# Sums of x's squares: from channel-major tiles with GpSimd additions to token-major tiles with ScalarE's accumulator, in one layer of a three-branch decoder block

## The chip, the cores and the metric

The kernel runs on one core of a Trainium2 chip. The metric is device time in microseconds (us). The time before is 1533.58 us, the median of three runs (1532.06 to 1534.87).

## The reference, cut to what matters

One decoder layer over 512 tokens of width 2048: RMSNorm of x, one wide projection `w_in`, three token mixers (sliding-window attention A, forgetting attention B, cross-attention C into 256 normalised memory tokens), gates, a merge and an output projection, all in float32.

```python
def rms_norm(x, gain):
    x32 = x.astype(jnp.float32)
    y = x32 * lax.rsqrt(jnp.mean(x32 * x32, axis=-1, keepdims=True) + EPS)
    return (y * gain.astype(jnp.float32)).astype(x.dtype)
...
    hn = rms_norm(x, norm_gain)
    proj = hn @ w_in
    (qa, ka, va, za, qb, kb, vb, zb, fb, qc, zc, gate_logits) = jnp.split(proj, IN_OFFSETS, axis=-1)
...
    mkv = rms_norm(mem, mem_norm_gain) @ w_mem_kv
...
    y = g[:, :, 0] * ua + g[:, :, 1] * ub + g[:, :, 2] * uc
    return x + y @ w_out
```

What the change touches is the mean of x's squares per token, and when the things around it happen.

## The kernel before, in words

**Tiling.** Every float32 product is made of three matmuls on split operands: high part times high part, high times low, low times high. For x the high part is `ah` (ScalarE, `x_part`, L307) and the low part `al` (VectorE, L308); for a weight tile `wa` the high part is `wb` (ScalarE, L195) and the low part `wc` (VectorE, L198). Both x and the weights come from DRAM on the queue of SyncE (SP).

**Units.** The projection runs in column chunks: qB, kB and vB of the first half of branch B come first, then others. A chunk is eight units; a unit is 256 of the 2048 channels: 24 matmuls of 384 columns (396 in kB, which carries the forget gates too). In the eight units of qB, unit u also brings x's tile `xraw` for its channels (`load_x`, channel-major: 128 channels by 512 tokens, twice). `xraw` has three buffers, `wa`, `wb` and `wc` two each. Gain is applied with x; the factor 1/rms of a token (`rstd`) is applied later, on what comes out of the projection, so the matmuls do not wait for it.

**Order.** PE, VectorE, ScalarE and GpSimd execute in the order in which the program is written. A clock counts half a slot for three matmuls, so that a unit is 4 slots; `later(dt, f)` and `at_slot(t, f)` put f's instructions into the order when that clock is reached. qB takes slots 0 to 32, kB 32 to 64, vB 64 to 96. The load of unit u+1 (`st.load`) is written at the start of unit u. SyncE's queue is ordered by the compiler's scheduler; each of its transfers waits for its buffer, and those behind it wait too.

**Sums of squares.** In each unit of qB ScalarE squares the whole `xraw` tile into `xsq` (L340) and GpSimd adds it to the accumulator `acc` (L341). `x_norm` at slot 36.5 sums `acc` over partitions with small matmuls against a column of ones (`x_ss`, L350) and takes the power -1/2. `x_rows` (slot 52) spreads `rstd` into rows (`rstdb`). `mem_norm` squares the memory's token-major tiles on ScalarE with its accumulator (`accum_out`, L373). `late_constants`, at slot 20, issues the loads of gains, sinks, the bias table and the like, 14 small transfers. `plan_sums` (slot 58 on) builds combinations of x's quarters (`x3s` to `x6s`, VectorE L1003, L1006, L1021) for a later stage.

Of the kernel before, what the change touches and what calls it, by code (L numbers as in the profile page):

```python
# [19 lines left out]
P = 128  # L20
# [23 lines left out]
def tile_hybrid_block(ctx, tc, xT, x, memT, mem, ng, mng, w_in, b_forget, gqa, gka, sinks, gqb, gkb, gqc, gkc,  # L44
# [41 lines left out]
    ac.activation(relt[:, :8], mhalf, AF.Exp)  # L86

    def late_constants():
        sy.dma_start(out=mngt, in_=mng)
        sy.dma_start(out=bfor, in_=b_forget.partition_broadcast(P))  # L90
        sy.dma_start(out=nsink, in_=sinks.partition_broadcast(P))
        later(20, lambda: po.tensor_scalar(nsink, nsink, -1.0, None, op0=ALU.mult))
        sy.dma_start(out=relt, in_=relm)
        for name, g, d in (("qa", gqa, 64), ("ka", gka, 64), ("qb", gqb, 64), ("kb", gkb, 64), ("qc", gqc, 128), ("kc", gkc, 128)):
            t = cp.tile([P, 1], F32, name=f"g_{name}")
            for o in range(0, P, d):
                sy.dma_start(out=t[o:o + d, :], in_=g)
            if name[0] == "q":
                t2 = cp.tile([P, 1], F32, name=f"gs_{name}")
                later(20, lambda t=t, t2=t2, d=d: ve.tensor_scalar(t2, t, float(np.float32(d) ** np.float32(-0.5)), None,  # L100
                                                                   op0=ALU.mult))
                t = t2
            gains[name] = t

    nsink = cp.tile([P, 12], F32, name="nsink")
    bfor = cp.tile([P, 12], F32, name="bfor")
# [15 lines left out]
    def at_slot(t, f):  # L122

        heapq.heappush(agenda, (t, next(seq), f))

    def later(dt, f):
        at_slot(clock[0] + dt, f)
# [172 lines left out]
    early = tc.tile_pool(name="early", bufs=1)  # L300
    earlyp = early.__enter__()

    acc = earlyp.tile([P, UK, S], F32, name="acc")

    def x_part(u, t, k):
        g = ngt[:, u * UK + k:u * UK + k + 1]
        ac.activation(ah[u][:, k, :], t[:, k, :], AF.Copy, scale=g)  # L307
# [3 lines left out]
    def first_unit(segs):  # L311

        (w, c0, n), = segs
        raw, h, l = w_tile("a", F32), w_tile("b"), w_tile("c")
        t = earlyp.tile([P, UK, S], F32, tag="xraw", bufs=3, name="xraw0")
        res = []
        for k in range(UK):
            sy.dma_start(out=t[:, k, :], in_=xT[k * P:(k + 1) * P, :])
            sy.dma_start(out=raw[:, k, :n], in_=w[k * P:(k + 1) * P, c0:c0 + n])
        for k in range(UK):  # L320
            hi, lo = h[:, k, :], l[:, k, :]
            low = x_part(0, t, k)
            ve.tensor_copy(hi[:, :n], raw[:, k, :n])
            ve.tensor_sub(lo[:, :n], raw[:, k, :n], f32(hi[:, :n]))
            low()
            res.append((hi, lo, n))
        later(1, lambda: ac.activation(acc, t, AF.Square))
        return res

    def load_x(u):  # L330
        if u == 0:
            return
        t = earlyp.tile([P, UK, S], F32, tag="xraw", bufs=3, name=f"xraw{u}")
        sy.dma_start(out=t, in_=xT[u * UK * P:(u + 1) * UK * P, :].rearrange("(k p) n -> p k n", p=P))
        for k in range(UK):
            x_part(u, t, k)()
        sq = earlyp.tile([P, UK, S], F32, tag="xsq", bufs=2, name=f"xsq{u}")

        def square():
            ac.activation(sq, t, AF.Square)  # L340
            po.tensor_tensor(acc, acc, sq, op=ALU.add)  # L341
        later(1.5, square)

    def x_norm():
        ones = earlyp.tile([P, 2], F32, name="ones")
        po.memset(ones, 1.0)
        b = sbank("x_ss")
        ve.tensor_tensor(acc[:, 0, :], acc[:, 0, :], acc[:, 1, :], op=ALU.add)
        for t in range(NT):
            pe.matmul(b[:, 2 * t:2 * t + 2], acc[:, 0, t * P:(t + 1) * P], ones, start=(t == 0), stop=(t == NT - 1))  # L350
        v = earlyp.tile([P, NT], F32, name="v_x")
        ve.tensor_scalar(v, b[:, :2 * NT].rearrange("p (t c) -> p t c", c=2)[:, :, 0], 1.0 / D, EPS, op0=ALU.mult, op1=ALU.add)
        power(rstd, v, NT)
        later(2, lambda: ve.scalar_tensor_tensor(out=rstd2, in0=rstd, scalar=1.0 / 64, in1=rstd, op0=ALU.mult, op1=ALU.mult))

    def x_rows():
        bb = earlyp.tile([P, NT, P], F32, name="rstd_cols")
# [6 lines left out]
    def power(out_ap, v, n):  # L364
        po.tensor_tensor(out_ap, v, mhalf[:, :n], op=ALU.pow)

    def mem_norm(t0):
        ss = earlyp.tile([P, 2, 2], F32, name="ss_m")

        def load(t, c):  # L370
            r = earlyp.tile([P, 1024], F32, tag="xtok", bufs=2, name=f"xt{t}{c}")
            sy.dma_start(out=r, in_=mem[t * P:(t + 1) * P, c * 1024:(c + 1) * 1024])
            later(10, lambda: ac.activation(r, r, AF.Square, accum_out=ss[:, t, c:c + 1]))  # L373

        def finish():
            v = earlyp.tile([P, 2], F32, name="v_m")
            ve.tensor_tensor(v, ss[:, :, 0], ss[:, :, 1], op=ALU.add)
            ve.tensor_scalar(v, v, 1.0 / D, EPS, op0=ALU.mult, op1=ALU.add)
            power(mrstd, v, 2)
        for k in range(4):  # L380
            at_slot(t0 + 6 * k, lambda k=k: load(k // 2, k % 2))
        at_slot(t0 + 32, finish)


    def qk_tile(name, tag, n, bufs):
# [30 lines left out]
    def evac_qk(key, tag, n, hd, bufs, scale=rstd, nt=NT, after=None, wait=0.5):  # L416

        nh = n // hd
        state = {}

        def f(b, pb, c0=0):
            if after is not None:
                after(b, pb)
            if b == 0:
                state["t"] = tokp.tile([P, nt, n], F32, tag=tag, bufs=bufs, name=f"t_{key}")
            t = state["t"]
            if scale is None:
                ac.copy(t[:, b, :], pb[:, c0:c0 + n])
            else:
                ac.activation(t[:, b, :], pb[:, c0:c0 + n], AF.Copy, scale=scale[:, b:b + 1])  # L430
            normalise(t[:, b, :], nh, hd, f"{key}{b}", wait, b if scale is None else None)
            if b == nt - 1:
                toks[key] = t
        return f
# [80 lines left out]
    def sbank(name):  # L515
        return bank(1, name)
# [331 lines left out]
    def b_chunks(part):  # L848
        c = part * 384
        st.add(f"qB{part}", [(w_in, QB + c, 384)], "tok", act_x, KT,  # L850
               evac_qk(f"qB{part}", "tq", 384, 64, 2, **({} if part else {"scale": None, "wait": 12})),
               None if part else load_x)
        segs = [(w_in, KB + c, 384)] + ([] if part else [(w_in, FB, 12)])
        st.add(f"kB{part}", segs, "tok", act_x, KT, evac_qk(f"kB{part}", "tk", 384, 64, 1, after=None if part else evac_f))
        st.add(f"vB{part}", [(w_in, VB + c, 384)], "tok", act_x, KT, evac_v(f"vB{part}", 6))
# [152 lines left out]
    def plan_sums(t0):  # L1008


        def one(u, n):
            xa, xb = (place(i, f"x{i}s{u}").rearrange("p k (t n) -> p (k t) n", t=2) for i in (n, n + 1))
            a, s1, s2, d = (xa[:, i, :] for i in range(4))
            s3, c, s4, b = (xb[:, i, :] for i in range(4))
            rows = [slice((2 * u + k) * P, (2 * u + k + 1) * P) for k in range(2)]
            halves = [slice(0, 256), slice(256, 512)]
            for dst, k, h in ((a, 0, 0), (b, 0, 1), (c, 1, 0), (d, 1, 1)):
                sy.dma_start(out=dst, in_=xT[rows[k], halves[h]])

            def norm(dst, k, h):  # L1020
                ve.scalar_tensor_tensor(out=dst, in0=dst, scalar=ngt[:, 2 * u + k:2 * u + k + 1],  # L1021
                                        in1=rstdb[:, halves[h]], op0=ALU.mult, op1=ALU.mult)

            def store():
                r = slice(u * P, (u + 1) * P)
                sy.dma_start(out=xad[r, :].rearrange("p (k n) -> p k n", n=256), in_=xa)
                sy.dma_start(out=xbd[r, :].rearrange("p (k n) -> p k n", n=256), in_=xb[:, 0:3, :])
            steps = [lambda: (norm(a, 0, 0), norm(b, 0, 1)), lambda: (norm(c, 1, 0), norm(d, 1, 1)),
                     lambda: (add(s1, b, d), sub(s2, s1, a)), lambda: (sub(s3, a, b), sub(s4, c, s2)), store]
            for i, f in enumerate(steps):  # L1030
                later(5.5 + 1.5 * i, f)
        for u in range(NP):
            at_slot(t0 + (0, 9, 18, 27, 44, 72, 100, 128)[u], lambda u=u: one(u, 3 + 2 * (u % 2)))
# [405 lines left out]
    for _ in range(5):  # L1439
        pe.matmul(wb, wz[:, :P], wz, start=True, stop=True)  # L1440
    st.load(1)
    at_slot(20, late_constants)
    at_slot(36.5, x_norm)
    run(0, 8)
    mem_norm(clock[0] + 4)
    later(20, x_rows)
    plan_sums(clock[0] + 26)
    run(8, n_p1)
    early.__exit__(None, None, None)
    atp = tc.tile_pool(name="at", bufs=1)  # L1450
    at.p = atp.__enter__()
# [64 lines left out]
```

## Time and profile before

| what | value |
|---|---|
| median of three runs | 1533.58 us |
| the profiled execution: its own time | 1534.17 us |
| the profiled execution: its span in the trace | 1532.4 us |
| PE busy in the span | 1492.3 us (97%) |
| VectorE (DVE), ScalarE (ACT), GpSimd (POOL) busy | 1083.6, 721.6, 272.0 us |
| chain that ended last | PE 73%, DVE 11%, ACT 6%, DMA 5% |

The span is what the trace covers; the execution's own time is 1.8 us longer, and that execution lies 0.6 us over the median. Busy times of PE are modelled ends of pipelined matmuls, so a wait read between two starts is a little longer than the idle time that a row names.

### The profile page before, as it was taken

The page shows a single profiled execution, that of the slowest core. Times are in us where ns is not written, and L with a number is a line of the kernel's source. Part 1 is how long each engine was busy: PE and PEld are TensorE (multiplying, and loading weights), DVE is VectorE, ACT ScalarE, POOL GpSimd, SP SyncE. Part 2 cuts the span into 40 slices and gives each one's busy share as a digit, 9 for nine tenths or more (in the row PEclk, how much of TensorE's full clock was granted, in tenths as well). Part 3 has the DMA queues.
Part 4 walks back from the last instruction along what each step waited for, and adds up shares of the span by engine and source line. Part 5 has one row for each costly group of instructions (what it writes and reads, how often), then busy time and mean ns, then how long its engine had stood idle before and what let it go on. Part 6 is the DMA issues. An engine that isn't in the chain of part 4 may idle for free.

```text
span 1532.4 us, 20507 instructions
## 1 busy us (share of the span) xinstructions
PE 1492.3 (97%) x7233; PEld 1273.4 (83%) x7233; DVE 1083.6 (71%) x1818; ACT 721.6 (47%) x1198; POOL 272.0 (18%) x295
## 2 busy tenths in 40 slices
PE   8999999999999999999999999999999999999998
PEld 7999999998877888888887878787878788887876
DVE  7576765663577764568878877777777556589987
ACT  5434654663566654454444444435355322245432
POOL 3323760662225431200000000000000101110000
PEclk9999999999999999999999999999999999999999
DMA  6656433223244322476666676767676756567583
GB/s 198 172 187 207 122 109 111 84 76 93 83 146 158 99 72 78 162 235 210 210 202 221 206 230 197 243 192 246 193 228 208 278 194 198 173 229 259 191 294 140
DMA packets 125264, 273.23 MB, mean 178 GB/s; under 512 B 13916, under 2 KB 52956, under 8 KB 125160
## 3 DMA queue, kind: packets, MB, share of 16 engines
q1 hardware_dynamic: 120984, 257.22, 52.6%
q10 hardware_dynamic: 4176, 14.69, 3.0%
q8 instruction: 57, 0.93, 0.2%
q14 instruction: 47, 0.39, 0.1%
HBM read 240.39 MB, written 31.48 MB: 177 GB/s over the span
## 4 chain that ended last, share of the span: by engine, by line
PE 73%; DVE 11%; ACT 6%; DMA 5%; issue 3%; POOL 1%; ACTq 1%; SPq 0%; DVEq 0%; POOLq 0%
PE P L1069 27%; PE z L284 11%; PE uA L1069 4%; PE qA L284 4%; PE kB L284 3%; PE qB L284 3%; PE uB L1069 3%; PE kvA L284 3%; PE uC L1069 3%; DMA rawl<-in_w_in_dram 3%; PE qC L284 3%; PE vB L284 2%; DVE R L1003 2%; DVE rawl L1006 2%; DVE wd L1112 2%
## 5 line engine op out<-in xcount | busy, mean ns | idle before, releaser
L1109 ACT CAST wa<-rawl 128x1024 fp32r<-128x1024 f32 x128 | 134.7, 1052 | 256.2 <-PE P L1069 140.1
L198 DVE TENSOR_TENSOR wc<-wa,wb 128x512 fp32r<-128x512 f32 (+2 forms) x254 | 162.0, 664 | 109.3 <-ACT wb L195 108.7
L195 ACT CAST wb<-wa 128x512 fp32r<-128x512 f32 (+2 forms) x254 | 131.3, 565 | 143.8 <-PE z L284 48.3
L1006 DVE TENSOR_TENSOR rawl<-rawl 128x512 f32<-128x512 f32 x256 | 176.6, 690 | 26.6 <-DMA rawl<-in_w_in_dram 16.5
L1112 DVE TENSOR_TENSOR wc<-rawl,wa 128x1024 fp32r<-128x1024 f32 x128 | 156.3, 1221 | 50.8 <-ACT wa L1109 50.7
L1350 POOL TENSOR_TENSOR y<-y,gA 128x512 f32<-128x512 f32 x16 | 24.8, 1559 | 701.0 <-DVE gA L1348 700.4
L1109 ACT CAST wb<-rawl 128x512 fp32r<-128x512 f32 (+1 forms) x128 | 107.1, 837 | 74.7 <-PE P L1069 51.7
L1112 DVE TENSOR_TENSOR wd<-rawl,wb 128x512 fp32r<-128x512 f32 (+1 forms) x128 | 121.8, 952 | 12.9 <-ACT wb L1109 12.7
L284 PE MATMUL z<-ah,wb 128*128 128x512 f32 x256 | 102.2, 399 | 0.0
L284 PE MATMUL z<-ah,wc 128*128 128x512 f32 x256 | 100.0, 391 | 0.0
L284 PE MATMUL z<-al,wb 128*128 128x512 f32 x256 | 99.8, 390 | 0.0
L1069 PE MATMUL P<-wd,xhx 128*128 128x512 f32 x192 | 76.5, 398 | 4.0 <-DVE wd L1112 3.6
L1069 PE MATMUL P<-wb,xhx 128*128 128x512 f32 x192 | 75.9, 395 | 1.8 <-ACT wb L1109 1.0
L1069 PE MATMUL P<-wb,xlx 128*128 128x512 f32 x192 | 74.9, 390 | 0.0
L1069 PE MATMUL P<-wa,xlx 128*128 128x512 f32 x192 | 74.7, 389 | 0.0
L1069 PE MATMUL P<-wa,xhx 128*128 128x512 f32 x192 | 74.7, 389 | 0.0
L1069 PE MATMUL P<-wa,yhx 128*128 128x512 f32 x192 | 74.7, 389 | 0.0
L1069 PE MATMUL P<-wa,ylx 128*128 128x512 f32 x192 | 74.7, 389 | 0.0
L1069 PE MATMUL P<-wc,yhx 128*128 128x512 f32 x192 | 74.7, 389 | 0.0
L1069 PE MATMUL P<-wc,xhx 128*128 128x512 f32 x192 | 74.7, 389 | 0.0
L1003 DVE TENSOR_TENSOR R<-P,R 128x512 f32<-128x512 f32 x88 | 56.1, 684 | 20.6 <-PE P L1069 20.2
L574 POOL TENSOR_SCALAR pB<-pB,denB 128x128 f32<-128x128 f32 (+3 forms) x48 | 56.1, 1169 | 49.1 <-DVE denB L573 34.5
(384 smaller groups left out, 4022.1 us busy)
## 6 DMA issues: line engine op xcount, KB each, us to landing
rawl<-in_w_in_dram SPq DMA_DIRECT2D x144, 512.0 KB, 4.4
rawl<-in_w_out_dram SPq DMA_DIRECT2D x48, 512.0 KB, 4.7
wa<-in_w_in_dram SPq DMA_DIRECT2D x63, 384.0 KB, 3.3
wa<-in_w_in_dram SPq DMA_DIRECT2D x64, 256.0 KB, 3.1
rawl<-in_w_in_dram SPq DMA_DIRECT2D x48, 256.0 KB, 4.2
gates<-R ACTq DMA_DIRECT2D x24, 512.0 KB, 7.9
wa<-in_w_in_dram SPq DMA_DIRECT2D x16, 512.0 KB, 3.7
wa<-in_w_mem_dram SPq DMA_DIRECT2D x16, 512.0 KB, 3.4
```

The source lines that it names most:

```text
L195: ac.copy(hi[:, :n], raw[:, i, :n])
L198: ve.tensor_sub(lo[:, :n], raw[:, i, :n], f32(hi[:, :n]))
L284: pe.matmul(pb, a, m, start=b in fresh, stop=last and not todo[b])
L574: po.tensor_scalar(p, p, den[:, 4 + i:5 + i], None, op0=ALU.mult)
L1003: ve.tensor_tensor(out, a, b, op=ALU.add)
L1006: ve.tensor_tensor(out, a, b, op=ALU.subtract)
L1069: pe.matmul(*args, **kw)
L1109: ac.copy(hi[:, :k, :], src)
L1112: return lambda: ve.tensor_tensor(lo[:, :k, :], src, f32(hi[:, :k, :]), op=ALU.subtract)
L1350: po.tensor_tensor(y, y, g, op=ALU.add)
```

## The change

The squares leave the qB units: `acc`, `xsq`, GpSimd's additions and the small matmuls are gone. Instead eight token-major tiles of x (128 tokens by 1024 channels, `xt`, four buffers) are loaded from the row-major x, one every 3 slots from slot 20, and ScalarE squares each 6 slots later with its accumulator (`square_sums`); `root` adds the two halves per token at slot 49. `late_constants` goes from slot 20 to slot 40 and spreads its loads, 3 slots apart. `mem_norm` goes from slot 36 to 60, `x_rows` from 52 to 56, `plan_sums` from 58 to 60, and the normalisation of qB's output waits 25 slots instead of 12.

```diff
@@ -86,21 +86,24 @@
     ac.activation(relt[:, :8], mhalf, AF.Exp)
 
     def late_constants():
-        sy.dma_start(out=mngt, in_=mng)
-        sy.dma_start(out=bfor, in_=b_forget.partition_broadcast(P))
-        sy.dma_start(out=nsink, in_=sinks.partition_broadcast(P))
-        later(20, lambda: po.tensor_scalar(nsink, nsink, -1.0, None, op0=ALU.mult))
-        sy.dma_start(out=relt, in_=relm)
-        for name, g, d in (("qa", gqa, 64), ("ka", gka, 64), ("qb", gqb, 64), ("kb", gkb, 64), ("qc", gqc, 128), ("kc", gkc, 128)):
+        def gain(name, g, d):
             t = cp.tile([P, 1], F32, name=f"g_{name}")
             for o in range(0, P, d):
                 sy.dma_start(out=t[o:o + d, :], in_=g)
             if name[0] == "q":
                 t2 = cp.tile([P, 1], F32, name=f"gs_{name}")
-                later(20, lambda t=t, t2=t2, d=d: ve.tensor_scalar(t2, t, float(np.float32(d) ** np.float32(-0.5)), None,
-                                                                   op0=ALU.mult))
+                later(8, lambda t=t, t2=t2: ve.tensor_scalar(t2, t, float(np.float32(d) ** np.float32(-0.5)), None, op0=ALU.mult))
                 t = t2
             gains[name] = t
+
+        steps = [lambda: sy.dma_start(out=bfor, in_=b_forget.partition_broadcast(P))]
+        steps += [lambda a=a: gain(*a) for a in (("qb", gqb, 64), ("kb", gkb, 64))]
+        steps += [lambda: sy.dma_start(out=nsink, in_=sinks.partition_broadcast(P)),
+                  lambda: sy.dma_start(out=relt, in_=relm), lambda: sy.dma_start(out=mngt, in_=mng),
+                  lambda: po.tensor_scalar(nsink, nsink, -1.0, None, op0=ALU.mult)]
+        steps += [lambda a=a: gain(*a) for a in (("qa", gqa, 64), ("ka", gka, 64), ("qc", gqc, 128), ("kc", gkc, 128))]
+        for i, f in enumerate(steps):
+            later(3 * i, f)
 
     nsink = cp.tile([P, 12], F32, name="nsink")
     bfor = cp.tile([P, 12], F32, name="bfor")
@@ -300,8 +303,6 @@
     early = tc.tile_pool(name="early", bufs=1)
     earlyp = early.__enter__()
 
-    acc = earlyp.tile([P, UK, S], F32, name="acc")
-
     def x_part(u, t, k):
         g = ngt[:, u * UK + k:u * UK + k + 1]
         ac.activation(ah[u][:, k, :], t[:, k, :], AF.Copy, scale=g)
@@ -324,7 +325,6 @@
             ve.tensor_sub(lo[:, :n], raw[:, k, :n], f32(hi[:, :n]))
             low()
             res.append((hi, lo, n))
-        later(1, lambda: ac.activation(acc, t, AF.Square))
         return res
 
     def load_x(u):
@@ -334,24 +334,26 @@
         sy.dma_start(out=t, in_=xT[u * UK * P:(u + 1) * UK * P, :].rearrange("(k p) n -> p k n", p=P))
         for k in range(UK):
             x_part(u, t, k)()
-        sq = earlyp.tile([P, UK, S], F32, tag="xsq", bufs=2, name=f"xsq{u}")
-
-        def square():
-            ac.activation(sq, t, AF.Square)
-            po.tensor_tensor(acc, acc, sq, op=ALU.add)
-        later(1.5, square)
-
-    def x_norm():
-        ones = earlyp.tile([P, 2], F32, name="ones")
-        po.memset(ones, 1.0)
-        b = sbank("x_ss")
-        ve.tensor_tensor(acc[:, 0, :], acc[:, 0, :], acc[:, 1, :], op=ALU.add)
-        for t in range(NT):
-            pe.matmul(b[:, 2 * t:2 * t + 2], acc[:, 0, t * P:(t + 1) * P], ones, start=(t == 0), stop=(t == NT - 1))
-        v = earlyp.tile([P, NT], F32, name="v_x")
-        ve.tensor_scalar(v, b[:, :2 * NT].rearrange("p (t c) -> p t c", c=2)[:, :, 0], 1.0 / D, EPS, op0=ALU.mult, op1=ALU.add)
-        power(rstd, v, NT)
-        later(2, lambda: ve.scalar_tensor_tensor(out=rstd2, in0=rstd, scalar=1.0 / 64, in1=rstd, op0=ALU.mult, op1=ALU.mult))
+
+    def square_sums(src, t, c, ss):
+
+        r = earlyp.tile([P, 1024], F32, tag="xtok", bufs=4, name=f"xt{t}{c}")
+        sy.dma_start(out=r, in_=src[t * P:(t + 1) * P, c * 1024:(c + 1) * 1024])
+        later(6, lambda: ac.activation(r, r, AF.Square, accum_out=ss[:, t, c:c + 1]))
+
+    def root(ss, out_ap, n):
+        v = earlyp.tile([P, n], F32, name=f"v_{n}")
+        ve.tensor_tensor(v, ss[:, :, 0], ss[:, :, 1], op=ALU.add)
+        ve.tensor_scalar(v, v, 1.0 / D, EPS, op0=ALU.mult, op1=ALU.add)
+        power(out_ap, v, n)
+
+    def x_norm(t0):
+        ss = earlyp.tile([P, NT, 2], F32, name="ss_x")
+        for n in range(2 * NT):
+            at_slot(t0 + 3 * n, lambda n=n: square_sums(x, n // 2, n % 2, ss))
+        at_slot(t0 + 6 * NT + 5, lambda: root(ss, rstd, NT))
+        at_slot(t0 + 6 * NT + 7, lambda: ve.scalar_tensor_tensor(out=rstd2, in0=rstd, scalar=1.0 / 64, in1=rstd, op0=ALU.mult,
+                                                                 op1=ALU.mult))
 
     def x_rows():
         bb = earlyp.tile([P, NT, P], F32, name="rstd_cols")
@@ -366,20 +368,9 @@
 
     def mem_norm(t0):
         ss = earlyp.tile([P, 2, 2], F32, name="ss_m")
-
-        def load(t, c):
-            r = earlyp.tile([P, 1024], F32, tag="xtok", bufs=2, name=f"xt{t}{c}")
-            sy.dma_start(out=r, in_=mem[t * P:(t + 1) * P, c * 1024:(c + 1) * 1024])
-            later(10, lambda: ac.activation(r, r, AF.Square, accum_out=ss[:, t, c:c + 1]))
-
-        def finish():
-            v = earlyp.tile([P, 2], F32, name="v_m")
-            ve.tensor_tensor(v, ss[:, :, 0], ss[:, :, 1], op=ALU.add)
-            ve.tensor_scalar(v, v, 1.0 / D, EPS, op0=ALU.mult, op1=ALU.add)
-            power(mrstd, v, 2)
         for k in range(4):
-            at_slot(t0 + 6 * k, lambda k=k: load(k // 2, k % 2))
-        at_slot(t0 + 32, finish)
+            at_slot(t0 + 4 * k, lambda k=k: square_sums(mem, k // 2, k % 2, ss))
+        at_slot(t0 + 24, lambda: root(ss, mrstd, 2))
 
 
     def qk_tile(name, tag, n, bufs):
@@ -848,7 +839,7 @@
     def b_chunks(part):
         c = part * 384
         st.add(f"qB{part}", [(w_in, QB + c, 384)], "tok", act_x, KT,
-               evac_qk(f"qB{part}", "tq", 384, 64, 2, **({} if part else {"scale": None, "wait": 12})),
+               evac_qk(f"qB{part}", "tq", 384, 64, 2, **({} if part else {"scale": None, "wait": 25})),
                None if part else load_x)
         segs = [(w_in, KB + c, 384)] + ([] if part else [(w_in, FB, 12)])
         st.add(f"kB{part}", segs, "tok", act_x, KT, evac_qk(f"kB{part}", "tk", 384, 64, 1, after=None if part else evac_f))
@@ -1439,13 +1430,12 @@
     for _ in range(5):
         pe.matmul(wb, wz[:, :P], wz, start=True, stop=True)
     st.load(1)
-    at_slot(20, late_constants)
-    at_slot(36.5, x_norm)
-    run(0, 8)
-    mem_norm(clock[0] + 4)
-    later(20, x_rows)
-    plan_sums(clock[0] + 26)
-    run(8, n_p1)
+    at_slot(40, late_constants)
+    x_norm(20)
+    at_slot(56, x_rows)
+    mem_norm(60)
+    plan_sums(60)
+    run(0, n_p1)
     early.__exit__(None, None, None)
     atp = tc.tile_pool(name="at", bufs=1)
     at.p = atp.__enter__()
```

How the order moves, at three places. First ScalarE, in the program before, in the second and third unit of qB (`ah` x's high part, `wb` the weights' high part, `xsq` the squares):

```order
L307 ACTIVATE ah_74<-xraw_136,ngt 128x512 x2
L195 CAST wb_145<-wa_143 128x384 x2
L327 ACTIVATE acc<-xraw_123 128x1024
L340 ACTIVATE xsq_142<-xraw_136 128x1024
L307 ACTIVATE ah_75<-xraw_182,ngt 128x512 x2
L195 CAST wb_191<-wa_189 128x384 x2
```

and of the change, from the seventh unit of qB to the first of kB:

```order
L308 ACTIVATE ah_79<-xraw_333,ngt 128x512 x2
L198 CAST wb_341<-wa_339 128x384 x2
L308 ACTIVATE ah_80<-xraw_373,ngt 128x512 x2
L198 CAST wb_381<-wa_379 128x384 x2
L342 ACTIVATE xt_331,ss_x<-xt_331 128x1024
L198 CAST wb_417<-wa_414 128x396 x2
```

Ahead of those rows the changed ScalarE holds only `ah` and `wb` rows; the squares of x begin behind the last `wb` of qB, from other tiles, `xt`.

Then SyncE's queue, in the program before, from the sixth unit's weights on (`nsink`, `relt` and `g_` are the constants, `xraw` x's channel-major tiles, `wa` weights):

```order
L185 DMA wa_312<-in_w_in_dram 128x2x384
L91 DMA nsink<-in_sinks_dram 128x12
L93 DMA relt<-in_relm_dram 128x256
L97 DMA g_qa<-in_gqa_dram 64x1 x2
L97 DMA g_ka<-in_gka_dram 64x1 x2
L97 DMA g_qb<-in_gqb_dram 64x1 x2
L97 DMA g_kb<-in_gkb_dram 64x1 x2
L97 DMA g_qc<-in_gqc_dram 128x1
L97 DMA g_kc<-in_gkc_dram 128x1
L334 DMA xraw_369<-in_xT_dram 128x2x512
L185 DMA wa_376<-in_w_in_dram 128x2x384
L334 DMA xraw_410<-in_xT_dram 128x2x512
```

and in the change, from the same weights on:

```order
L188 DMA wa_299<-in_w_in_dram 128x2x384
L341 DMA xt_331<-in_x_dram 128x1024
L334 DMA xraw_333<-in_xT_dram 128x2x512
L188 DMA wa_339<-in_w_in_dram 128x2x384
L341 DMA xt_365<-in_x_dram 128x1024
L334 DMA xraw_373<-in_xT_dram 128x2x512
L188 DMA wa_379<-in_w_in_dram 128x2x384
L341 DMA xt_399<-in_x_dram 128x1024
L188 DMA wa_414<-in_w_in_dram 128x2x384
L188 DMA wa_414<-in_w_in_dram 128x2x12
L341 DMA xt_431<-in_x_dram 128x1024
```

The twelve constant transfers ahead of x's seventh tile (`xraw_369`) are behind all of qB's loads now, and single loads of token-major x stand between the loads of qB.

Last VectorE, where kB ends and vB begins (`nr_kB` and `t_kB` normalise kB's output, `fl` the forget logits, `x3s` and `x4s` x's first combinations); before:

```order
L1021 SCALAR_TENSOR_TENSOR x3s_781<-x3s_781,ngt,rstdb 128x256
L1021 SCALAR_TENSOR_TENSOR x4s_782<-x4s_782,ngt,rstdb 128x256
L456 SCALAR_TENSOR_TENSOR fl<-kB_3_507,rstds,bfor 128x12
L409 TENSOR_TENSOR t_kB_814<-t_kB_814,nr_kB_816 128x384
L402 TENSOR_REDUCE nr_kB_842<-sq_kB_846 128x6
L403 TENSOR_SCALAR nr_kB_842<-nr_kB_842 128x6
L198 TENSOR_TENSOR wc_867<-wa_804,wb_866 128x384
```

and in the change:

```order
L394 TENSOR_SCALAR nr_kB_818<-nr_kB_818 128x6
L201 TENSOR_TENSOR wc_845<-wa_776,wb_844 128x384
L400 TENSOR_TENSOR t_kB_786<-t_kB_786,nr_kB_804 128x384
L393 TENSOR_REDUCE nr_kB_832<-sq_kB_842 128x6
L394 TENSOR_SCALAR nr_kB_832<-nr_kB_832 128x6
L201 TENSOR_TENSOR wc_845<-wa_776,wb_844 128x384
L1012 SCALAR_TENSOR_TENSOR x3s_766<-x3s_766,ngt,rstdb 128x256
L1012 SCALAR_TENSOR_TENSOR x4s_767<-x4s_767,ngt,rstdb 128x256
```

The first `x3s` and `x4s` rows stood ahead of the second vB unit's weights (`wc`) and stand behind both halves of them now.

## Rows read from the trace of the kernel before

**Rows 1.** Windows: busy us (instructions) per engine, clock, DMA share, GB/s.

```profile
0.00:50.00 50.00, 40.44 (x202) 37.60 (x203) 35.15 (x38) 28.32 (x47) 18.61 (x15) 0.97 0.63 195
50.00:100.00 50.00, 49.16 (x280) 48.51 (x279) 30.52 (x85) 20.41 (x43) 14.07 (x12) 1.00 0.51 148
```

**Rows 2.** Waits of PE over the whole trace: us, times, longest.

```profile
PE qB L284 <- DVE wc L198: 6.6, 4, 3.3
...
PE vB L284 <- DVE wc L198: 0.8, 1, 0.8
```

**Rows 3.** Timeline of PE in qB: start, us, what [idle before <- releaser].

```profile
14.82 0.34 PE L284 MATMUL qB<-wb,ah 128*128 128x384 f32 x1
...
18.47 0.44 PE L284 MATMUL qB<-wc,ah 128*128 128x384 f32 x1 [3.31 <-DVE wc L198]
...
19.79 0.47 PE L284 MATMUL qB<-wb,al 128*128 128x384 f32 x1
...
23.25 0.34 PE L284 MATMUL qB<-wc,ah 128*128 128x384 f32 x1
...
36.44 0.34 PE L284 MATMUL qB<-wb,al 128*128 128x384 f32 x1
37.37 0.44 PE L284 MATMUL qB<-wb,ah 128*128 128x384 f32 x1 [0.60 <-ACT wb L195]
38.28 0.44 PE L284 MATMUL qB<-wc,ah 128*128 128x384 f32 x1 [0.46 <-DVE wc L198]
...
45.13 0.44 PE L284 MATMUL qB<-wc,ah 128*128 128x384 f32 x1 [2.40 <-DVE wc L198]
...
49.23 0.34 PE L284 MATMUL kB<-wb,ah 128*128 128x396 f32 x1
```

**Rows 4.** Timeline of DVE in qB.

```profile
6.49 0.56 DVE L324 TENSOR_TENSOR wc<-wa,wb 128x384 fp32r<-128x384 f32 x1
...
12.74 3.05 DVE L308 SCALAR_TENSOR_TENSOR al<-xraw,ngt,ah 128x512 fp32r<-128x512 f32 x2 [1.60 <-ACT ah L307]
15.71 5.37 DVE L198 TENSOR_TENSOR wc<-wa,wb 128x384 fp32r<-128x384 f32 x2
21.00 1.40 DVE L308 SCALAR_TENSOR_TENSOR al<-xraw,ngt,ah 128x512 fp32r<-128x512 f32 x2
...
42.37 4.13 DVE L198 TENSOR_TENSOR wc<-wa,wb 128x384 fp32r<-128x384 f32 x4
```

**Rows 5.** Timeline of POOL in qB.

```profile
15.24 2.75 POOL L341 TENSOR_TENSOR acc<-acc,xsq 128x1024 f32<-128x1024 f32 x1 [0.67 <-ACT xsq L340]
18.23 2.43 POOL L341 TENSOR_TENSOR acc<-acc,xsq 128x1024 f32<-128x1024 f32 x1 [0.23 <-ACT xsq L340]
...
41.84 2.82 POOL L341 TENSOR_TENSOR acc<-acc,xsq 128x1024 f32<-128x1024 f32 x1 [0.60 <-ACT xsq L340]
```

**Rows 6.** Windows of 2 us in qB, columns as in rows 1.

```profile
6.00:8.00 2.00, 2.00 (x13) 2.00 (x12) 1.58 (x3) 0.00 (x0) 0.00 (x0) 1.00 1.04 372
...
20.00:22.00 2.00, 2.00 (x8) 1.89 (x8) 2.00 (x3) 0.00 (x0) 0.66 (x1) 0.50 0.00 0
```

**Rows 7.** Timeline of SyncE's queue (transfers issued).

```profile
31.09 0.43 SPq L97 DMA_DIRECT2D g_kc<-in_gkc_dram  x1
31.63 0.38 SPq L334 DMA_DIRECT2D xraw<-in_xT_dram  x1
```

**Rows 8.** Timeline of ACT: in qB, and one of the memory's squares in kB.

```profile
13.22 0.91 ACT L195 CAST wb<-wa 128x384 fp32r<-128x384 f32 x2
...
35.58 1.34 ACT L307 ACTIVATE ah<-xraw,ngt 128x512 fp32r<-128x512 f32 x2 [5.20 <-DMA xraw<-in_xT_dram]
...
64.12 1.05 ACT L373 ACTIVATE xt<-xt 128x1024 f32<-128x1024 f32 x1
```

**Rows 9.** The chain that ended last, in order of time, in kB: start, us, what.

```profile
54.24 0.79 PE x_ss L350 x8
```

**Rows 10.** The longest landing of x's tiles, from the view of tile xraw.

```profile
DMA to landing us min/median/max: 3.0/4.6/6.7
```

## The prediction

> **What bounds the kernel now.** I read the windows first. From 50 us on the core is a matmul stream with few holes: in 50 to 100 us PE is busy 49.16 of 50. The first 50 us are the poor stretch: PE busy 40.44, mean granted clock 0.97, while the transfers move 195 GB/s on average [rows 1]. This stretch is the chunk qB, the only one in which x comes in with the weights. Next the waits of PE: in qB it waited 6.6 us in four places for `wc`, the low parts that VectorE makes of the weights [rows 2]. Then the timeline of PE, to price the holes. Between 23.25 and 36.44 nothing waits, and 76 matmuls start in it: 0.1736 us each, so 4.17 us for a unit of 24. The first matmul of qB's third unit starts at 14.82, the first of kB at 49.23: 34.4 us for six units that need 144 x 0.1736 = 25.0. So 9.4 us are lost there [rows 3]. They are:
>
> - 3.5 us ahead of 18.47 (the matmul before started at 14.82 and needs 0.17).
> - 1.55 us of low clock: the eleven starts from 19.79 to 23.25 take 3.46 us instead of 1.91 [rows 3]. The granted clock is 0.50 in 20 to 22 us, the lower of the two levels (1.2 GHz instead of 2.4) [rows 6], right after PE had stood still for 3.5 us.
> - 1.5 us at 37.37 and 38.28 (0.93 + 0.91 less two matmuls).
> - 2.4 us ahead of 45.13 by its note, and 0.5 us of restarts behind the waits.
>
> Why `wc` is late is seen on VectorE and GpSimd side by side. One half of `wc` takes 0.56 us at 6.49, two of `al` 1.40 us at 21.00. But the two halves at 15.71 take 5.37 us together, and two of `al` at 12.74 take 3.05 [rows 4]. GpSimd's additions of the squares run from 15.24 to 17.99 and from 18.23 to 20.66, and the matmul that needs the first half starts at 18.47, half a microsecond behind the end of the first addition [rows 3, 5]. The same at 42.37: four halves take 4.13 us, of which the first one sits under the addition of 41.84 to 44.66, and PE waits until 45.13 [rows 3 to 5]. So VectorE's two-input operations stand still while GpSimd adds, and PE stands behind VectorE.
>
> The 1.5 us at 37 to 38 us have another cause: SyncE issued constants until 31.52 and x's seventh tile only at 31.63 [rows 7]; ScalarE sat 5.2 us until it landed, and the cast of the weights behind it was late with it [rows 8].
>
> **The change, part by part.** *GpSimd's additions go.* Nothing else of GpSimd stands in qB, so VectorE works there at its undisturbed durations. Is it in time? For the third unit a bound comes from before: the high part of its weights began at 13.22 without any wait [rows 8], behind three squares that are gone too. So its first half is there by 13.7 at the latest, its low half 0.56 later, at 14.3. PE needs it at 14.82 + 0.17 = 15.0. The 3.5 us go, the low clock that followed goes with them, and so do the 2.4 us at 45.13: 7.9 us with the restarts.
>
> *The constants leave qB's queue.* X's seventh tile then waits only for the weights ahead of it, and the 1.5 us go. In kB the fourteen transfers take about 0.43 us of SyncE each [rows 7], 6 us in some 33; the forget bias is written 24 slots ahead of its use, the sinks 9 slots (9.4 us) ahead of GpSimd's negation, against 6.7 us for the longest landing of a full x tile [rows 10]. I cost them at nothing. If the sinks came late, GpSimd's powers for qB would be held, but the output they scale is used only behind slot 96.
>
> *Later units of qB.* A weight load may start when VectorE is through with the tile of two units before, 1.5 us (0.91 cast, 0.56 subtraction) into the unit three ahead of its use, and must have landed 1.5 us ahead of its own unit: 12.5 - 3.0 = 9.5 us for a landing, where the longest of x's was 6.7 [rows 10]. So no new wait in the steady state.
>
> *Eight token-major tiles of x.* They add 8 x 512 KB = 4.19 MB. In three of qB's units one is loaded beside x and weights: 0.92 + 0.52 = 1.44 MB. With a full queue the transfers move 372 GB/s [rows 6], so 3.9 us of the 4.17. Tight, but hidden. The squares (8 x 1.05 us [rows 8], as many as were removed) now lie in ScalarE's order between kB's casts. The tightest place is slot 32: an evacuation of about 0.5, a square 1.05, half a cast 0.46, a subtraction 0.56, together 2.6 of 4.17 us. Nothing on the path; without that cover at most 8.4 us.
>
> *The small matmuls of `x_ss` go*: 0.8 us of PE [rows 9], a sure gain, since PE has no hole there. `root` needs two small VectorE operations and one power as before.
>
> *Memory norms, `x_rows`, x's combinations.* `x_rows` costs PE the same four slots later. At vB's start PE waited 0.8 us for `wc` [rows 2], because the memory's square and x's first combination stood ahead of it. The order now has them behind both halves of `wc`, but the combinations come two slots nearer to the forget gates' long chain. Between a gain of all 0.8 and a loss of two slots, 12 x 0.1736 = 2.1 us, I take a gain of 0.4.
>
> **Sum.** 9.4 (qB) + 0.8 (`x_ss`) + 0.4 (vB) = 10.6 us. Behind it PE is the stream that sets the time and every buffer is freed by its progress, so the shift should reach the end whole. From the profiled execution's 1534.17 that gives 1523.6; that execution lies 0.6 over the median, so 1523.0 us, 0.7% less. A measurement of this kernel can tell about 0.2%, 3.1 us, from no change.
>
> **Rivals.**
>
> - *The wait moves to VectorE's crowd at slots 64 to 80.* For it: before, PE waited there already. Against: the order puts `wc` first. Two slots lost: 1525.5. Chance 0.10.
> - *The added transfers gate qB's last units.* For it: the mean over the first 50 us is 195 GB/s, not 372 [rows 1]. At 195 a unit needs 7.4 us, three of them fall 9.7 us behind, of which the spare 2.8 us (9.5 - 6.7) are free: 6.9 lost, 1529.9. It decides below some 283 GB/s (1.44 MB in 5.1 us). Against: the mean contains stretches in which the queue was blocked, such as 20 to 22 us with nothing moved [rows 6]. Chance 0.07.
> - *VectorE was slow because of the transfers, not of GpSimd.* Then only 1.5 + 0.8 are gained: 1531.3, no change that can be told. Against: at 6.49 `wc` took its 0.56 us in a window with the transfers full (1.04), and in 20 to 22 us, with no transfer at all, VectorE's second half still ended only behind GpSimd's addition [rows 4 to 6]. Chance 0.03. The Trainium skill, SBUF — State Buffer, section "SBUF: two separate sides", says that VectorE and GpSimd hold one port pair exclusively for a whole instruction, a VectorE operation with two SBUF inputs against a GpSimd one that reads SBUF, and that transfers cannot contend with engines there. By that rule all the 7.9 us go; without it, next to none. The trace agrees: `wc` ended 0.5 us behind the addition's end.
> - *Slower: SyncE's queue is held by the new tiles.* There are four buffers, so the fifth to eighth tile wait, at the head of the queue, for squares that stand in ScalarE's order behind qB's evacuations and kB's casts, and kB's weights wait behind them. If each of the four held the weights for a unit, 4 x 4.17 = 16.7 us would be lost: 1539.7. It decides from 2.6 us at each of the four. Against: the fifth waits for a square at slot 26, 10 slots ahead of the first use of weights behind it. Chance 0.04.
>
> **How the numbers follow.** The forecast has 0.76; its own range is 1521 to 1525.5: between all terms at their best (9.4 + 0.8 + 0.8, 1522.6) and a qB that keeps 1.4 us of its holes with nothing at vB (8.8, 1524.8), and the runs before spread 1.4 us to both sides. With the first rival and a part of the second, the range is 1521 to 1527.5; 0.14 and less lie outside. Faster by over 0.2% (under 1530.5): 0.76 + 0.10 + half of the second rival, 0.90. Within 0.2%: 0.06. Slower: 0.04.
>
> **What would show it.** In the trace after: one half of `wc` at about 0.56 us everywhere in qB; third unit of qB starting near 14.8 and kB's first matmul near 39.8 instead of 49.23; a granted clock of 1.00 through 10 to 40 us; x's seventh tile issued by about 22 us; no PE wait at kB over half a microsecond. The prediction is wrong if PE waits for `ah` or `wb` behind a transfer in qB, if the clock still falls to 0.50 in it, or if kB starts near 40 us and the end still comes at the old time: then something behind gave the gain back.

## The result, and the profile after

The change takes 1522.38 us in the median (1521.38 to 1523.74, four runs) against 1532.82 us for the kernel before on the same chip (1529.55 to 1534.87, four runs): a ratio of 0.9934, 95% interval 0.9916 to 0.9951. The forecast was 1523.0. The profiled execution took 1523.03 us, its span is 1521.1 us.

Windows of the change, with the columns of [rows 1]; the two of 2 and 10 us lie where the clock had fallen before [rows 6]:

```profile
0.00:50.00 50.00, 47.29 (x253) 45.51 (x254) 24.70 (x44) 29.48 (x55) 0.73 (x7) 1.00 0.83 270
50.00:100.00 50.00, 49.41 (x282) 47.97 (x281) 35.07 (x101) 23.32 (x49) 14.54 (x14) 1.00 0.68 203
20.00:22.00 2.00, 2.00 (x14) 2.00 (x13) 1.99 (x4) 1.55 (x3) 0.00 (x0) 1.00 1.02 322
20.00:30.00 10.00, 10.00 (x60) 10.00 (x59) 6.55 (x12) 5.98 (x11) 0.00 (x0) 1.00 0.97 348
```

In the first 50 us PE gains 6.85 us of work, with 51 more matmuls. VectorE's busy time falls by 10.45 us, though in qB it does nearly the same work. Its operations are shorter. GpSimd is all but idle, the granted clock is 1.00, and 20 to 22 us, where nothing was transferred before, now moves 322 GB/s.

VectorE of the change in qB and at kB's end, as in [rows 4]:

```profile
12.57 1.02 DVE L201 TENSOR_TENSOR wc<-wa,wb 128x384 fp32r<-128x384 f32 x2
16.60 1.03 DVE L201 TENSOR_TENSOR wc<-wa,wb 128x384 fp32r<-128x384 f32 x2 [1.05 <-ACT wb L198]
...
73.00 0.23 DVE L399 TENSOR_SCALAR nr_qB<-nr_qB,rstds 128x6 f32<-128x6 f32 x1 [0.71 <-POOL nr_qB L367]
73.27 0.56 DVE L400 TENSOR_TENSOR t_qB<-t_qB,nr_qB 128x384 f32<-128x384 f32 x1
73.74 0.55 DVE L201 TENSOR_TENSOR wc<-wa,wb 128x384 fp32r<-128x384 f32 x1
74.21 0.23 DVE L447 SCALAR_TENSOR_TENSOR fl<-kB,rstds,bfor 128x12 f32<-128x12 f32 x1
```

Two halves of `wc` took 5.37 us at 15.71 before; they take 1.02 now. VectorE waits for ScalarE there (1.05 us at 16.60), and from the third unit on PE waits for nothing in qB. PE of the change, as in [rows 3], with the starts of qB's third unit, of kB and of vB:

```profile
15.02 0.33 PE L287 MATMUL qB<-wb,ah 128*128 128x384 f32 x1
...
39.98 0.34 PE L287 MATMUL kB<-wb,ah 128*128 128x396 f32 x1
...
75.42 0.34 PE L287 MATMUL vB<-wb,ah 128*128 128x384 f32 x1
76.19 0.44 PE L287 MATMUL vB<-wb,ah 128*128 128x384 f32 x1
77.26 0.44 PE L287 MATMUL vB<-wb,ah 128*128 128x384 f32 x1 [0.27 <-ACT t_kB L421]
78.29 0.44 PE L287 MATMUL vB<-wb,ah 128*128 128x384 f32 x1 [0.23 <-ACT t_kB L421]
```

From the first matmul of qB's third unit to kB it is 24.96 us, where the count of matmuls gave 25.0: nothing is lost there any more. The table follows four places through the program: where kB, vB, the next q chunk and the gates' product stage start on PE, and the end of the span.

| us | kB | vB | next q | product | end |
|---|---|---|---|---|---|
| before | 49.23 | 85.56 | 121.35 | 714.2 | 1532.4 |
| change | 39.98 | 75.42 | 111.17 | 703.6 | 1521.1 |
| gained up to here | 9.25 | 10.14 | 10.18 | 10.6 | 11.3 |

PE's waits for `wc` in qB, 6.6 us before [rows 2], are one of 0.5, and new ones for `t_kB` stand in vB:

```profile
PE vB L287 <- ACT t_kB L421: 0.5, 2, 0.3
PE qB L287 <- DVE wc L201: 0.5, 1, 0.5
```

So 9.25 us come from qB, 0.89 from kB, 0.04 from vB. All of it passes on to the end; a further 1.1 us come behind the next q chunk, 0.7 of them in the product stage, which the change doesn't touch, and are looked at below.

### The profile page after: what moved, and what is told of

Same layout as the page of the kernel before. It is cut to its first block, busy times and chain, and to the rows that moved or that the text cites. A ratio compares the mean times of both kernels' runs of the same rounds, so it can differ in the third digit from the quotient of the medians.

```text
span 1521.1 us, 20494 instructions
## 1 busy us (share of the span) xinstructions
PE 1489.0 (98%) x7225; PEld 1271.1 (84%) x7225; DVE 1070.3 (70%) x1818; ACT 722.9 (48%) x1206; POOL 252.0 (17%) x287
## 4 chain that ended last, share of the span: by engine, by line
PE 76%; DVE 9%; ACT 6%; DMA 4%; issue 2%; POOL 1%; ACTq 1%; SPq 0%; DVEq 0%; POOLq 0%
PE P L1060 28%; PE z L287 11%; PE uA L1060 4%; PE qA L287 4%; PE qB L287 4%; PE vB L287 4%; PE kB L287 3%; PE uB L1060 3%; PE kvA L287 3%; PE uC L1060 3%; PE qC L287 3%; DVE R L994 2%; DVE rawl L997 2%; ACT R L1244 2%; DVE wd L1103 2%
## 5 line engine op out<-in xcount | busy, mean ns | idle before, releaser
L201 DVE TENSOR_TENSOR wc<-wa,wb 128x512 fp32r<-128x512 f32 (+2 forms) x254 | 153.3, 630 | 119.7 <-ACT wb L198 119.1
```

Source lines behind the costliest of these rows:

```text
L201: ve.tensor_sub(lo[:, :n], raw[:, i, :n], f32(hi[:, :n]))
```

## The experiments

My theory was that of the prediction: GpSimd's additions hold VectorE (7.9 us), constants hold SyncE's queue (1.5 us). The rivals were that GpSimd is harmless and the new order of loads brought the gain, and that the added row loads are only just hidden.

**The additions alone**, taken out of the kernel before:

```diff
             ac.activation(sq, t, AF.Square)
-            po.tensor_tensor(acc, acc, sq, op=ALU.add)
```

> The kernel before with GpSimd's additions of the squares left out (so the norm of x comes from the first unit's squares alone); ScalarE's squares, the small matmuls and the early constants stay. Theory: VectorE stood behind GpSimd. Then one half of wc takes 0.56 us throughout qB, and kB's first matmul comes 7.9 us earlier (41.3 instead of 49.2) if the constants cost their 1.5 us on their own, or up to 9.4 us earlier (39.8) if the constants only hurt because the queue was already late; the time falls by as much, to 1523.5 to 1525 us. Rival, transfers slowed VectorE: wc at 15.71 still takes over 5 us for two halves, kB starts at 49, time as before.

Measured: 1523.01 us (1522.82 to 1523.52), ratio 0.9925 [0.9905, 0.9944]. By its time alone this kernel can't be told from the whole change (0.9934). In the trace it can: kB starts at 40.88, so 8.35 us of the change's 9.25 are here. VectorE and the rest of what the constants cost, in the timelines of VectorE, PE, SyncE's queue and ScalarE:

```profile
13.77 1.02 DVE L198 TENSOR_TENSOR wc<-wa,wb 128x384 fp32r<-128x384 f32 x2
...
32.62 0.44 PE L284 MATMUL qB<-wc,ah 128*128 128x384 f32 x1 [0.46 <-DVE wc L198]
...
25.68 0.43 SPq L97 DMA_DIRECT2D g_kc<-in_gkc_dram  x1
26.22 0.38 SPq L334 DMA_DIRECT2D xraw<-in_xT_dram  x1
...
29.93 1.34 ACT L307 ACTIVATE ah<-xraw,ngt 128x512 fp32r<-128x512 f32 x2 [4.71 <-DMA xraw<-in_xT_dram]
```

The last constant is again issued right ahead of x's seventh tile, ScalarE waits 4.71 us for that tile, and PE still loses about 1.0 us (0.26 at 31.72 and 0.72 at 32.62). Everything else is gone.

**The constants alone**, `late_constants` as the change has it and at slot 40, in the kernel before:

```diff
-    at_slot(20, late_constants)
+    at_slot(40, late_constants)
```

> The kernel before with the constants alone issued as in the change (from slot 40, spread); GpSimd's additions stay. Theory: the holes at 37.37 and 38.28 close, 1.5 us; the waits at 18.47 and 45.13 and the low clock stay; kB starts near 47.7, time 1.5 us lower. Rival, the constants are what made the whole of qB late: kB starts near 40, time 9 us lower. If the constants do not matter at all: kB at 49.2.

Measured: 1528.98 us (1526.94 to 1531.33, ten runs), ratio 0.9969 [0.9957, 0.9981]; kB at 46.67, 2.56 us earlier, more than the 1.5 I expected. PE, and windows of 2 us:

```profile
18.35 0.69 PE L287 MATMUL qB<-wc,ah 128*128 128x384 f32 x1 [3.31 <-DVE wc L201]
...
43.09 0.45 PE L287 MATMUL qB<-wc,ah 128*128 128x384 f32 x1 [0.42 <-DVE wc L201]
```

```profile
18.00:20.00 2.00, 1.65 (x5) 1.65 (x6) 2.00 (x3) 1.61 (x3) 1.47 (x1) 0.50 0.12 11
20.00:22.00 2.00, 2.00 (x7) 2.00 (x7) 2.00 (x2) 0.00 (x0) 1.00 (x1) 0.50 0.86 275
22.00:24.00 2.00, 2.00 (x8) 2.00 (x8) 2.00 (x5) 0.00 (x0) 0.00 (x0) 0.50 0.45 173
```

The first stall and the low clock behind it stay, so they don't come from the constants. But the wait of 2.40 us at 45.13 [rows 3] is down to 0.42, although the additions are all there. That wait needed both: the late tile and an addition in the way. Alone, the two parts give 8.35 and 2.56, together 9.25, so some 1.7 us can be had by either. From the third unit's first matmul to kB they give 8.34, 2.45 and 9.45. And the low clock lasted longer in this run than in the kernel before: 17 starts from 18.84 to 24.27 take 5.43 us, 2.5 more than at the full clock, against 1.55 for the eleven before. Without that the constants alone would give about 0.9 more, and the shared part would be about 2.3 us, nearly the whole wait of 2.40. Why the clock stayed low longer is open.

**Additions put back** into the change, seven useless ones that read x's high parts:

```diff
+        later(1.5, lambda: po.tensor_tensor(acc, acc, f32(ah[u]), op=ALU.add))
```

> The changed kernel with seven GpSimd additions of 128x1024 put back into qB, as work without use: each adds the high part of x's tile to an accumulator that nobody reads. No square, buffer or transfer changes. Theory: GpSimd's additions are what held VectorE: halves of wc or al of 2 us and more return, PE waits for wc again, kB starts 5 to 8 us later than 39.98, and the time is 5 to 8 us above 1522.4. Rival, GpSimd was harmless and the freed buffers, the squares or the constants made the gain: kB at 40, time 1522.

Measured: 1526.46 us (1525.94 to 1528.22, five runs), ratio to the kernel before 0.9951 [0.9932, 0.9970]; kB at 44.08, 4.1 us later than in the change. VectorE, GpSimd and PE:

```profile
9.79 5.39 DVE L201 TENSOR_TENSOR wc<-wa,wb 128x384 fp32r<-128x384 f32 x2
...
9.19 5.58 POOL L340 TENSOR_TENSOR acc<-acc,ah 128x1024 f32<-128x1024 f32 x2 [6.92 <-ACT ah L311]
...
12.57 0.44 PE L287 MATMUL qB<-wc,ah 128*128 128x384 f32 x1 [1.97 <-DVE wc L201]
...
19.16 0.44 PE L287 MATMUL qB<-wc,ah 128*128 128x384 f32 x1 [1.54 <-DVE wc L201]
```

The 5.4 us for two halves of `wc` are back, beside two additions of 5.58 us together, with SyncE's queue as the change has it. So it is not the order of loads. The loss is less than I expected: these additions wait only for `ah`, start earlier, and later ones meet `al`, which has more room. No wait reached 2 us, and the clock stayed at 1.00.

**GpSimd busy, but reading nothing.** The change, with ScalarE's squares back in the second to eighth unit, seven of them, and three memsets of GpSimd behind each:

```diff
+            ac.activation(sq, t, AF.Square)
+            for _ in range(3):
+                po.memset(sq, 0.0)
```

> The changed kernel with work without use in qB: ScalarE squares each of x's channel-major tiles as before, and GpSimd then writes zeros over the result three times instead of adding it to an accumulator, so that GpSimd is busy about 3 us a unit but reads nothing. Theory, only a GpSimd operation that reads holds VectorE's two-input operations: wc stays at 0.56 us a half, kB starts at 40 to 40.5. Rival, any GpSimd work on large tiles holds VectorE: halves of wc of 1 us and more, kB several us later.

Measured: 1524.33 us in a single run; kB at 39.45. GpSimd and VectorE:

```profile
14.83 8.99 POOL L342 MEMSET xsq<- 128x1024 f32 x9 [0.98 <-ACT xsq L340]
...
16.75 1.02 DVE L201 TENSOR_TENSOR wc<-wa,wb 128x384 fp32r<-128x384 f32 x2
18.42 1.41 DVE L309 SCALAR_TENSOR_TENSOR al<-xraw,ngt,ah 128x512 fp32r<-128x512 f32 x2 [0.65 <-ACT ah L308]
```

GpSimd is busy for 8.99 us with nine memsets, almost on end, and VectorE's durations don't move. So what holds VectorE is not GpSimd at work, but these additions, which read where the memsets only write. Not every GpSimd instruction that reads holds it, though. At vB's start of the change GpSimd takes four powers on end, each with two inputs in SBUF, but of six elements a partition. The third runs from 79.38 to 80.98 us (GpSimd's spans are rough in the profile), and a scaling of VectorE with two inputs takes 0.55 us in the midst of it, as one took 0.56 at 73.27 with GpSimd idle:

```profile
76.61 5.96 POOL L367 TENSOR_TENSOR nr_kB<-nr_kB,mhalf 128x6 f32<-128x6 f32 x4 [3.41 <-DVE fl L447]
...
79.70 0.55 DVE L400 TENSOR_TENSOR t_kB<-t_kB,nr_kB 128x384 f32<-128x384 f32 x1
```

Whether the amount read or the kind of the operation makes that difference, no run here shows. The squares on ScalarE cost qB nothing either.

**Row loads doubled.** The change, with every token-major tile of x loaded a second time:

```diff
+        if src is x:
+            r2 = earlyp.tile([P, 1024], F32, tag="xtok2", bufs=2, name=f"xu{t}{c}")
+            sy.dma_start(out=r2, in_=src[t * P:(t + 1) * P, c * 1024:(c + 1) * 1024])
```

> The changed kernel with each of the eight token-major tiles of x loaded a second time into buffers that nobody reads: 4.19 MB more. Theory, at 372 GB/s for a full queue: a unit of qB's last three needs 1.97 MB or 5.3 us of 4.17, falls 1.1 us behind each, 3.4 in all, of which 2.8 are spare: kB starts at 40.0 to 40.6 and the time is up by at most 1 us. Rival, the transfers run near the 195 GB/s of the mean: 10.1 us a unit, kB some 15 us later; then the single loads would have been near the limit too.

Measured: 1522.83 us (1522.67 to 1523.15), ratio 0.9923 [0.9904, 0.9943]; kB at 39.58. Windows:

```profile
20.00:30.00 10.00, 10.00 (x59) 10.00 (x59) 5.35 (x10) 4.42 (x8) 0.00 (x0) 1.00 1.02 364
30.00:40.00 10.00, 10.00 (x60) 10.00 (x59) 3.41 (x6) 6.54 (x14) 0.00 (x0) 1.00 1.02 390
```

The transfers are full (1.02) for 20 us, and PE has no hole. The rival that the row loads gate qB falls, and so does my own "tight".

**The waits at vB's start.** The change lost its 0.4 us there. In PE's timeline above, four first matmuls of vB's banks stand 0.77, 1.07 and 1.03 us apart, where vB's undisturbed ones stand 0.52 apart: 1.3 us. They wait for ScalarE to empty kB's banks (`t_kB`), and ScalarE waits for VectorE:

```profile
74.53 0.58 ACT L421 ACTIVATE t_kB<-kB,rstds 128x384 f32<-128x384 f32 x1 [2.30 <-DVE fl L447]
```

VectorE's rows of the change show why `fl` is late: qB's last scaling (L399, L400) waited until 73.00 for a power of GpSimd, and `wc` and `fl` stand behind it. The scaling stands there because its delay is 25 slots now. Shortening it:

```diff
-               evac_qk(f"qB{part}", "tq", 384, 64, 2, **({} if part else {"scale": None, "wait": 25})),
+               evac_qk(f"qB{part}", "tq", 384, 64, 2, **({} if part else {"scale": None, "wait": 22})),
```

> The changed kernel with the normalisation of qB's output 3 slots earlier (22 slots of wait instead of 25). In the changed kernel three matmuls at vB's start wait for ScalarE's evacuation of kB, 1.4 us with restarts, 0.3 before the change. Theory: the last scaling of qB's output stands in VectorE's order right ahead of the weights and forget logits at kB's end, waits for GpSimd's power, and so makes kB's evacuation late. Moved ahead, the three waits shrink to 0.3 us or less and the stretch from vB's first matmul to the next qB's falls from 35.75 us to 34.7 to 35.0; the whole by 0.7 to 1 us, less than the time can tell. Rival, the evacuation itself is too slow for the banks: the waits stay and the stretch stays at 35.7.

Measured: 1523.15 us (1521.28 to 1524.11), ratio 0.9938 [0.9921, 0.9954]. From vB to the next q it is 34.36 us instead of 35.75, and the waits at vB's start are gone, but from kB to vB 37.22 instead of 35.44. PE and VectorE:

```profile
67.12 1.13 PE L363 MATMUL rstd_rows<-ident,rstd_cols 128*128 128x128 f32 x8 [1.53 <-DVE rstd_cols L360]
...
66.56 0.42 DVE L360 COPY rstd_cols<-rstds 128x512 f32<-128x512 f32 x1
```

The scaling, moved up, now stands ahead of the copy for `x_rows` (L360), and PE waits for that copy. The wait had gone to another place, so the copy has to move as well:

```diff
-    at_slot(56, x_rows)
+    at_slot(52, x_rows)
```

> The changed kernel with two numbers different: qB's normalisation waits 22 slots, and the spreading of rstd into rows stands at slot 52 instead of 56, ahead of that normalisation in VectorE's order. Theory from the run with 22 slots alone: the waits at vB's start go (the stretch from vB's first matmul to the next qB's first is 34.4 us instead of 35.75), and the 1.7 us that PE then waited in kB for the copy of rstd go too, so kB to vB is 35.5 us again; 1.4 us less than the change in all, kB's start apart: a time of about 1521. Rival, rstd itself is not there at slot 52: PE waits for the copy in kB again, by 0.5 us or more, and part or all is lost.

Measured: 1522.32 us (1521.56 to 1523.58, five runs), ratio 0.9927 [0.9914, 0.9941]. From kB to vB 35.65, from vB to the next q 34.32: 69.97 us, against 71.19 in the change. The profile notes no PE wait between 12 and 111 us, and the span is 1519.3. In the trace this version is 1.2 us ahead of the change there; the timed runs can't tell the two apart.

**Both kernels once more**, unchanged, to see how much two executions of one kernel differ.

> The kernel before, unchanged, profiled again: a control. From the first product matmul of the gate stage (714.2 us in the trace before) to the end the profiled executions of the runs so far took 815.4 to 818.2 us although no edit touches that part. If that is noise of an execution, this one differs from 818.2 by a like amount while kB starts at 49.2 and vB at 85.6 again. If the stretch is 818.2 again within 0.3, the late part was changed by the edits.

> The changed kernel, unchanged, profiled again: a control. kB starts at 40.0 and vB at 75.4 within 0.5 us; the stretch from the first product matmul of the gate stage to the end was 817.5 us. If it moves by 1 us or more between two executions of one kernel, differences of that size between kernels there have no cause in the edits.

Measured: 1533.15 us for the kernel before (ratio to itself 1.0005 [0.9996, 1.0015]) and 1522.16 for the change (0.9935 [0.9920, 0.9950]). The start of kB repeats less well than I expected: 49.12 instead of 49.23 for the kernel before, but 39.24 instead of 39.98 for the change, 0.74 us earlier, where I had allowed 0.5; vB follows at 74.69. All of it arises ahead of qB's third unit, whose first matmul starts at 14.28 instead of 15.02. From there to kB it is 24.96 us in both executions of the change, and in the four runs with rows twice, memsets, wait 22, and wait 22 with rows at 52. So a difference of 0.7 us between two starts of kB needs no cause in the edits, and the stretch from the third unit to kB is the better measure: 34.41 and 34.16 us in the kernel before, 24.96 in the change.

From the start of the product stage to the end, which no edit touches, the spans are:

| kernel | product stage to end, us |
|---|---|
| before, two executions | 818.2, 818.2 |
| change, two executions | 817.5, 817.0 |
| additions alone; constants alone | 815.4, 815.6 |
| additions back; rows twice; wait 22 | 816.6, 817.8, 817.6 |
| memsets; wait 22 and rows at 52 | 819.1, 817.3 |

By the word of the expectation, that the kernel before comes to 818.2 again puts the differences down to the edits. I don't go so far. Inside that stretch the two executions of before part by up to 1.65 us (the last matmul of its tile `yt` starts at 1383.0 and at 1381.3) and meet again, and the two of the change differ by 0.5 at the end. The 2.6 to 2.8 us that the two partial kernels gained there stay unexplained. For this reason the experiments are read by the start of kB and its distance from the third unit, and their total times, lower than their part of qB gives, are not taken as a measure of the parts.

## Why the prediction was right, and where its terms were off

- **The sum.** 10.6 us were forecast up to the next q chunk; the trace shows 10.18 there, and 11.1 between the two profiled executions' own times. The remaining 0.9 us or so lie behind that chunk, most of them in the product stage, which the change doesn't touch and which took 815.4 to 819.1 us over kernels that don't differ there. So it is in part luck that the median, 1522.38, came so near to 1523.0: a term failed by 0.4, and a stretch that nobody changed gave more than that back.
- **GpSimd holds VectorE (7.9) and the constants hold the queue (1.5).** Their sum was right: 34.41 us less 24.96 from the third unit on, 9.45 of 9.4 (9.25 by kB's start, since the third unit started 0.20 later). The split was wrong in kind: I priced the 2.4 us at 45.13 as GpSimd's alone. Either part by itself removes most of it, as the two partial kernels show (8.35 and 2.56 us by kB's start). The bound for the third unit held: it starts at 15.02, and no PE wait follows in qB. (Ahead of the cast at 13.22 ScalarE had done two squares, not three; the bound doesn't hang on it.)
- **That GpSimd's additions hold VectorE** was argued from durations and is now shown from three sides: additions out, VectorE at its 1.02 us for two halves; additions in, 5.39; memsets in, 1.02. The Trainium skill, SBUF — State Buffer, section "SBUF: two separate sides", names the condition, a VectorE operation with two SBUF inputs against a GpSimd one that reads SBUF. The additions and the memsets agree with it; the powers at 76.61 read SBUF too and held nothing, so for them the measurement goes against it. No run here sets an addition against a VectorE operation with one input.
- **The low clock (1.55).** It went with its stall, as forecast. In the kernel before and with the constants alone, PE stood still for about 3.3 us and was then granted 0.50, the level of 1.2 GHz; behind the waits of 2.40 us or less, here and in [rows 3], it stayed at 1.00, 2.4 GHz.
- **The row loads and the constants in kB, costed at nothing.** Right. I called the loads tight at 3.9 of 4.17 us; twice as many are hidden too. The fear of a GB/s average, 195, was unfounded: that was a queue held up, not a limit. The queue rival, 16.7 us, didn't come: x's seventh tile was issued at 18.58 and the eighth at 21.90.
- **`x_ss` (0.8).** 0.89 from kB to vB.
- **vB (0.4).** The mis-sized term: 0.04. The old wait for `wc` did go, but three new ones came at vB's start. The step that failed is "If the sinks came late, GpSimd's powers for qB would be held, but the output they scale is used only behind slot 96". I asked who uses the output, not what stands behind its scaling in VectorE's order. That is `wc` and `fl`, and behind `fl` ScalarE and vB's banks. The sinks were not late: their negation, at 72.95, stands behind the power that the last scaling waited for, and the delay of 25 slots was enough. It is the first rival's kind of wait, at vB's first slots (64.5 to 65.5), and the term came out near nothing because the old wait for `wc` left at the same time.

## What to carry to other kernels

When an operation takes several times its usual duration, look at what the other engines execute in the same microseconds before looking at its inputs; here three runs (the neighbour out, back in, and replaced by one that reads nothing) settled it for the additions. Two causes that end in one wait can't be priced apart from one trace: the first to go takes the shared part with it. When the start of a program scatters, measure from a landmark behind the scatter. A delayed step whose result nobody needs yet still costs what stands behind it in its engine's order, so list those rows for each step that is moved.

## What the runs showed of the hardware that was not expected

- Nine GpSimd memsets, 8.99 us almost on end, held none of VectorE's two-input operations, while its additions, some 2.8 us each, stretched two of them from 1.02 to 5.4 us. Four of its powers, 5.96 us on end, read SBUF and didn't stretch the scaling beside them (0.55 us).
- With loads of x's rows doubled the transfers moved 364 and 390 GB/s over 10 us each, as much as 2 us with the transfers full before (372, [rows 6]), beside a PE without a hole.
- Untouched parts of one program start up to 1.65 us apart in two executions, and ends that agree can hide that.
